# One tile for both parts of the tokens, packed gate jobs, and another order of exponentials, silus and scans, in a hybrid SSD and RG-LRU block

## The chip, the cores and the metric

The kernel runs on one core of one Trainium2 chip. The metric is the device time of one execution in microseconds; of several runs the median is given.

## The reference, cut to what matters

One layer over 256 latent and 256 context tokens, 2048 channels, all in float32. Tokens are normalised, modulated and projected once; the projection feeds two mixers, whose outputs are merged by gates taken from the same normalised tokens.

```python
h = modulate(rmsnorm(x, norm_mix), sh_m, sc_m)          # the context tokens alike
z, xs, bs, cs, dt_raw, xr, yr = split(h @ w_in)
xs, bs, cs = silu(conv4([xs, bs, cs]))                  # depthwise, 4 taps
dt = softplus(dt_raw + bias)
y  = bidirectional_ssd(xs, dt, A, bs, cs)               # 4 groups of 8 heads, chunks of 128
o_s = rmsnorm(y * silu(z)) @ w_out_ssd
r, i = sigmoid(xr @ w_a + b_a), sigmoid(xr @ w_x + b_x) # per head of 128, both directions
a = exp(-8 * r * softplus(-lam))
u = sqrt(1 - a * a) * (i * xr)
r_out = linear_scan(a, u)                               # both directions
o_r = (r_out * gelu(yr)) @ w_out_lru
g_s, g_r = split(sigmoid(h @ w_gate + b_gate))
x = x + g_m * ((g_s * o_s + g_r * o_r) @ w_o)
x = x + g_f * swiglu(modulate(rmsnorm(x), sh_f, sc_f))
out = rmsnorm(x)
```

Only the scans' final states are taken from the context tokens. The gates, z and yr need latent tokens alone.

## The kernel before, in words

Channels lie on the partitions, tokens on the free axis. Every float32 product is made of parts in the faster float32r form: a value is split into a high part and a low part (the rest), for the tokens as for the weights, and three of the four partial products are summed in PSUM: high by high, high weight by low token, low weight by high token. `T1` holds the high parts of the 16 channel tiles, `T2` the low parts; in each, columns 0 to 255 are latent and 256 to 511 context tokens.

A `Job` is one block of 128 output channels, over 16 channel tiles (44 for the last FFN matrix). SP loads its weights in pieces of 8 tiles (512 KB), ACT rounds a piece to the high part (L173), DVE subtracts to the low part (L174); rings of four pieces. `product` issues the matmuls in one of these forms:
- "both": three matmuls of 512 columns for each tile (L188 to L190), latent and context;
- "lat": three of 256 columns (L192 to L194): the gate jobs (32) and the jobs of C (4);
- "packed": one of 512 columns, whose operand holds high and low parts of 256 tokens side by side, and one of 256 with the low weights (L206, L209), for z, yr, the output projections and the FFN. `halves` (L300) then adds the two halves of the PSUM bank: a copy on ACT, an add on DVE;
- "slab" (L228, L230): six FFN jobs together, and "last": the last job of a matrix.

For the packed form both parts have to lie in one tile. So, after the last job on context tokens, 16 DVE copies (L924, L925) put the low latent parts into the context half of `T1`.

The order of PE's work is written out: jobs in a list, and after each job the work that is due in its turn. `in_turn(n, f)` (L243) asks for `f` n turns later, 0 being the job under way; it is called from a job's evacuation, or from a turn (there, 0 is the next job). Besides, `step` (L287) takes the next entries of the list `bg` once per job. On ACT and DVE a planner orders instructions by estimated times and priorities; but `fn` (L105) keeps all of ACT's functions that need a table (Exp, Silu, Sigmoid, Sqrt, Tanh, Gelu) in the order in which the program calls them.

Stages: input and modulation (to about 146 us); gate jobs, two for each xr job, with the RG-LRU (`lru_batch`, two channel tiles per batch: operands, gates of the first tile, gates of the second, decays, scans) and the softplus of dt (`dt_evac`); four groups of SSD jobs, six jobs each (xs, C, xs, B, xs, xs); the last eight gate jobs, under which the last group is computed; z, yr, the output projections, w_o, FFN. 

Of an SSD group (`ssd_group`), after its last xs job: the silus of B, C and xs at once, in the evacuation (L705); then, by the tables LONG and SHORT (the last group), the transposes and states (`context_tokens` first), and four units (two half groups by two chunks), each with `fetch` (a broadcast DMA of cumulated decays, AC), `operands` (Exp of AC and of E, then G) and `products` (24 matmuls, L833). The unit of LONG's last column has its products in turn 7, that is one job after the next group's xs is complete. In `lru_batch` the scans of the batch before (Sqrt first, L555) have an entry of their own ahead of the gates.

LONG and SHORT (L692, L693) give, in this order, the turns of the three steps of the states, of the four products, fetches and operands; `todo` (L573) gives the entries of an RG-LRU batch, where an entry marked True is done together with the one behind it.

Of the kernel before, what the change touches and what calls it, by code (L numbers as in the profile page):

```python
# [14 lines left out]
P = 128  # L15
# [40 lines left out]
def hybrid_block(  # L56
# [38 lines left out]
    T1 = big.tile([P, KT, 2 * T], F32R, name="T1")  # L95
    T2 = big.tile([P, KT, 2 * T], F32R, name="T2")
# [80 lines left out]
    def product(job, after_piece):  # L177
# [5 lines left out]
        for k in range(job.kts):  # L183
            h, l = job.w[k // KP]
            wh, wl = h[:, k % KP, :], l[:, k % KP, :]
            s, e = k == 0, k == last
            if job.mode == "both":
                pe.matmul(ps, wh, T1[:, k, :], start=s, stop=False)  # L188
                pe.matmul(ps, wh, T2[:, k, :], start=False, stop=False)  # L189
                pe.matmul(ps, wl, T1[:, k, :], start=False, stop=e)  # L190
            elif job.mode == "lat":
                pe.matmul(ps[:, :T], wh, T1[:, k, :T], start=s, stop=False)  # L192
                pe.matmul(ps[:, :T], wh, T2[:, k, :T], start=False, stop=False)  # L193
                pe.matmul(ps[:, :T], wl, T1[:, k, :T], start=False, stop=e)  # L194
            elif job.mode == "narrow":

                pe.matmul(ps, wh, T1[:, k, :], start=s, stop=False)
                pe.matmul(ps, wh, T2[:, k, :], start=False, stop=e)
            elif job.mode == "last":
                a = job.act(k)  # L200
                pe.matmul(ps[:, :T], wh, a[:, :T], start=s, stop=False)
                pe.matmul(ps[:, :T], wh, a[:, T:], start=False, stop=False)
                pe.matmul(ps[:, :T], wl, a[:, :T], start=False, stop=e)
# [17 lines left out]
    def slab(job, after_piece):  # L221

        pss = [mm_ps("ps1") for _ in range(NF - 4)] + [ssd_ps("ps1") for _ in range(3)] + [lru_ps("ps1")]
        for k in range(KT):
            h, l = job.w[k]
            a = job.act(k)
            for n, ps in enumerate(pss):
                pe.matmul(ps, h[:, n, :], a, start=k == 0, stop=False, skip_group_check=True)  # L228
            for n, ps in enumerate(pss):
                pe.matmul(ps[:, T:], l[:, n, :], a[:, :T], start=False, stop=k == KT - 1, skip_group_check=True)  # L230
# [78 lines left out]
    def split(dst, src):  # L309

        act.copy(dst[:, :T], src)
        dve.tensor_sub(dst[:, T:], src, dst[:, :T].bitcast(F32))
# [196 lines left out]
    def lru_batch(tiles):  # L509
# [42 lines left out]
        def scans():  # L552
# [4 lines left out]
            for t in tiles:  # L557
# [15 lines left out]
        todo = [(False, [lambda: operands(t0)]), (False, before[:]), (False, [lambda: gates(t0), lambda: operands(t1)]),  # L573
                (False, []), (True, [lambda: gates(t1), decays])]
# [23 lines left out]
    def dt_evac(ps):  # L598
# [13 lines left out]
        def steps(part):  # L612
# [11 lines left out]
            if part == 0:  # L624
# [9 lines left out]
                fn(ex[:, :P], ex[:, :P], AF.Exp)  # L634
                dve.tensor_tensor(ex[f, :P], ex[f, :P], dt[f, 0:P], ALU.mult)
                dve.tensor_tensor(ex[b, :P], ex[b, :P], dt[b, P:2 * P], ALU.mult)
                cols = (dt[:, :P], dt[:, P:], ac[:, :P], ac[:, P:], ex[:, :P])
            else:
                scan(ex[f, :T - 1][:, ::-1], da[f, 1:][:, ::-1], T - 1, f)
                scan(ex[b, 1:], da[b, :T - 1], T - 1, b)  # L640
                fn(ex, ex, AF.Exp)
                dve.tensor_tensor(ex, ex, dt, ALU.mult)
                cols = (ex[:, :P], ex[:, P:])

# [66 lines left out]
    def ssd_group(g):  # L711
# [133 lines left out]
        return (silus, [context_tokens, context_states, carried_states], *zip(*units))  # L845
# [42 lines left out]
    def z_job(i):  # L888
        ys, pre = loads(yD[i])

        def f(ps):
# [5 lines left out]
            act.activation(T2[:, i, :T], t, AF.Copy, scale=g)  # L897
            dve.scalar_tensor_tensor(T2[:, i, T:], t, g, T2[:, i, :T].bitcast(F32), ALU.mult, ALU.subtract)
        return Job(w_z[i], KT, "packed", h_act, f, pre=pre)

    def yr_job(i):
        rs, pre = loads(rD[i])

        def f(ps):
# [3 lines left out]
            split(T3[:, i, :], t)  # L908
        return Job(w_yr[i], KT, "packed", h_act, f, pre=pre)

    def h_act(k):
        return T1[:, k, :]
# [4 lines left out]
    with tc.manual_schedule(engines={mybir.EngineType.PE}):  # L917
# [4 lines left out]


        for k in range(KT):  # L924
            dve.tensor_copy(T1[:, k, T:], T2[:, k, :T].bitcast(F32))  # L925
# [15 lines left out]
    def mix_jobs(n):  # L941
# [11 lines left out]
        def fr(ps):  # L953
# [3 lines left out]
            split(T1[:, n, :], t)  # L957

        return [Job(w_os[n], KT, "packed", lambda k: T2[:, k, :], fs, pre=pre),
                Job(w_ol[n], KT, "packed", lambda k: T3[:, k, :], fr)]  # L960
# [15 lines left out]
    def f_act(k):  # L976
        t = (T2, T3, T4)[k // KT]
        return t[:, k % KT, :]
# [44 lines left out]
    for k in range(KT):  # L1023
# [4 lines left out]
        dve.scalar_tensor_tensor(T1[:, k, T:], t, sh, T1[:, k, :T].bitcast(F32), ALU.add, ALU.subtract)  # L1028
# [94 lines left out]
```

## Time and profile before

| what | value |
|---|---|
| three runs | 2028.81, 2029.35, 2024.41 us, median 2028.81 |
| profiled execution | 2027.59 us, span 2025.8 us |
| PE busy | 1963.7 us, 97% |
| DVE busy | 1430.7 us, 71% |
| ACT busy | 1088.2 us, 54% |
| mean granted clock of PE | 0.986 of 2.4 GHz |
| ACT table loads | 48, 1283 ns each |

A matmul's listed duration holds its way through the array, which the next one overlaps; what one costs in a row of matmuls is the distance from start to start. A granted clock of 1.00 is 2.4 GHz, 0.50 is 1.2 GHz; a value between is a mix of both within the stretch. In a timeline's brackets stands the idle time of the engine ahead of an instruction, and what released it.

### The profile page before, as it was taken

The numbers are of one execution on the slowest core, as the hardware profiler recorded it, in microseconds if no ns is written. First come the engines' busy times: TensorE is split into PE (matmuls) and PEld (weight loads), VectorE is DVE, ScalarE is ACT, GpSimd is POOL, SyncE is SP. The second block draws the span as 40 slices with busy tenths as digits, with TensorE's granted clock in tenths as the row PEclk, the third lists the DMA queues.
The fourth block names the chain that finished last, engine by engine and source line by source line (L and its number), as shares of the span: only waits on it lengthen the run. The fifth ranks groups of instructions, "written<-read, shape, count | busy, mean of one in ns | idle before, by whom it ended". The sixth has DMA issues, their size and how long they took to land.

```text
span 2025.8 us, 30510 instructions
## 1 busy us (share of the span) xinstructions
PE 1963.7 (97%) x11633; PEld 1691.9 (84%) x11633; DVE 1430.7 (71%) x2153; ACT 1088.2 (54%) x1652; POOL 0.2 (0%) x4
## 2 busy tenths in 40 slices
PE   7999899999999879999999999899999999999997
PEld 3778898898878769888888888788888888888887
DVE  5578989886776666888777878776666665545544
ACT  4245878684564454766655544554444444444442
POOL 0000000000000000000000000000000000000000
PEclk9999999999999989999999999999999999999999
DMA  9974354556454457899888877577777776666663
GB/s 371 358 271 144 122 160 132 170 170 199 140 160 143 138 164 228 264 315 360 290 274 274 271 249 254 175 249 232 231 241 237 230 230 189 184 188 186 185 193 122
DMA packets 143842, 440.32 MB, mean 217 GB/s; under 512 B 17488, under 2 KB 36176, under 8 KB 143568
## 3 DMA queue, kind: packets, MB, share of 16 engines
q1 hardware_dynamic: 143328, 437.91, 66.4%
q8 instruction: 91, 1.49, 0.3%
q10 hardware_dynamic: 368, 0.47, 0.1%
q14 instruction: 55, 0.45, 0.1%
HBM read 427.77 MB, written 10.55 MB: 216 GB/s over the span
## 4 chain that ended last, share of the span: by engine, by line
PE 92%; DMA 2%; DVE 2%; ACT 2%; issue 1%; SPq 0%; DVEq 0%; ACTq 0%
PE ps L206 36%; PE ps L209 19%; PE ps L188 5%; PE ps L189 5%; PE ps L190 5%; PE ps L192 3%; PE ps L193 3%; PE ps L194 3%; DMA AC<-acD 1%; PE ps L391 1%; PE pa L344 1%; PE ps L392 1%; PE py L833 1%; PE ps L393 1%; PE ps L228 1%; PE lg L535 1%
## 5 line engine op out<-in xcount | busy, mean ns | idle before, releaser
L174 DVE TENSOR_TENSOR wl<-raw,wh 128x1024 fp32r<-128x1024 f32 (+1 forms) x566 | 677.8, 1200 | 386.9 <-ACT wh L173 382.3
L173 ACT CAST wh<-raw 128x1024 fp32r<-128x1024 f32 (+1 forms) x566 | 581.0, 1030 | 646.8 <-issue 221.4
L206 PE MATMUL ps<-T,wh 128*128 128x512 f32 x3236 | 814.7, 393 | 0.0
L206 PEld LDWEIGHTS ps<-T,wh 128*128 128x128 f32 x3236 | 581.6, 189 | 105.2 <-issue 0.7
L209 PEld LDWEIGHTS ps<-T,wl 128*128 128x128 f32 x3236 | 442.7, 190 | 33.3
L209 PE MATMUL ps<-T,wl 128*128 128x256 f32 x3236 | 452.9, 282 | 0.0
L188 PE MATMUL ps<-T,wh 128*128 128x512 f32 x464 | 184.2, 397 | 0.0
L189 PE MATMUL ps<-T,wh 128*128 128x512 f32 x464 | 180.9, 390 | 0.0
L190 PE MATMUL ps<-T,wl 128*128 128x512 f32 x464 | 180.6, 389 | 0.0
L473 DVE SCALAR_TENSOR_TENSOR rawa<-rawa,sc 128x1024 f32<-128x1024 f32 x128 | 153.1, 1222 | 28.4 <-DMA rawa<-in_dram 28.1
L192 PE MATMUL ps<-T,wh 128*128 128x256 f32 x576 | 165.4, 287 | 0.0
L193 PE MATMUL ps<-T,wh 128*128 128x256 f32 x576 | 163.7, 284 | 0.0
L194 PE MATMUL ps<-T,wl 128*128 128x256 f32 x576 | 163.6, 284 | 0.0
L192 PEld LDWEIGHTS ps<-T,wh 128*128 128x128 f32 x576 | 111.3, 193 | 1.9 <-issue 0.7
L193 PEld LDWEIGHTS ps<-T,wh 128*128 128x128 f32 x576 | 111.4, 193 | 1.2 <-issue 0.5
L194 PEld LDWEIGHTS ps<-T,wl 128*128 128x128 f32 x576 | 111.2, 193 | 0.0
L188 PEld LDWEIGHTS ps<-T,wh 128*128 128x128 f32 x464 | 87.1, 188 | 20.5 <-issue 2.3
L189 PEld LDWEIGHTS ps<-T,wh 128*128 128x128 f32 x464 | 87.2, 188 | 18.9 <-issue 1.4
L190 PEld LDWEIGHTS ps<-T,wl 128*128 128x128 f32 x464 | 87.1, 188 | 18.5
L107 ACT ACT_TABLE_LOAD x48 | 61.6, 1283 | 0.8
L804 ACT ACTIVATE E<-AC,wt 128x128 f32<-128x128 f32 x64 | 20.6, 391 | 61.8 <-DMA AC<-acD 61.8
L385 DVE TENSOR_TENSOR wl<-raw,wh 128x896 fp32r<-128x896 f32 x16 | 17.5, 1092 | 45.1 <-ACT wh L384 45.1
(236 smaller groups left out, 1881.8 us busy)
## 6 DMA issues: line engine op xcount, KB each, us to landing
raw<-in_dram SPq DMA_DIRECT2D x534, 512.0 KB, 4.5
rawa<-in_dram SPq DMA_DIRECT2D x128, 512.0 KB, 5.9
wa<-in_dram SPq DMA_DIRECT2D x64, 512.0 KB, 7.2
AC<-acD SPq DMA_DIRECT2D x16, 512.0 KB, 6.6
raw<-in_dram SPq DMA_DIRECT2D x16, 448.0 KB, 7.1
raw<-in_dram SPq DMA_DIRECT2D x16, 384.0 KB, 3.3
raw<-in_dram SPq DMA_DIRECT2D x18, 256.0 KB, 2.7
X<-in_dram SPq DMA_DIRECT2D x8, 512.0 KB, 7.2
```

Of the source, the lines that this page charges most:

```text
L107: i = act.activation(dst, src, func, **kw).ins
L173: act.copy(h[:, :n], raw[:, :n])
L174: held["low"] = dve.tensor_sub(l[:, :n], raw[:, :n], h[:, :n].bitcast(F32)).ins
L188: pe.matmul(ps, wh, T1[:, k, :], start=s, stop=False)
L189: pe.matmul(ps, wh, T2[:, k, :], start=False, stop=False)
L190: pe.matmul(ps, wl, T1[:, k, :], start=False, stop=e)
L192: pe.matmul(ps[:, :T], wh, T1[:, k, :T], start=s, stop=False)
L193: pe.matmul(ps[:, :T], wh, T2[:, k, :T], start=False, stop=False)
L194: pe.matmul(ps[:, :T], wl, T1[:, k, :T], start=False, stop=e)
L206: pe.matmul(ps, wh, job.act(k), start=s, stop=False, skip_group_check=True)
L209: pe.matmul(ps[:, T:], l[:, i % KP, :], job.act(i)[:, :T], start=False, stop=i == last, skip_group_check=True)
L473: i = dve.scalar_tensor_tensor(raw, raw, 1.0, sc[:, h * 1024:h * 1024 + 1024], ALU.mult, ALU.mult, accum_out=MP[:, n, h:h + 1]).ins
```

## The change

- `T1` and `T2` become the two halves of one tile `TT`. The packed form reads an operand of two strips of 256 columns, one in each half (`h_act`, `c_act`), in place of 512 adjacent columns; the matmul's output is still one bank of 512 columns.
- The gate jobs take the packed form, and `halves`. The 16 copies go. z's result is put into the context columns of both halves.
- An RG-LRU batch's scans come behind the next batch's gates of the first tile, in that entry, and no longer in the entry ahead.
- The dt work starts one turn later, and its exponentials and transposes get turns of their own.
- The silus of an SSD group move from the evacuation into turn 0, behind what that turn holds already; in the last group but one the fourth unit's products move from turn 7 to 8.

```diff
-    T1 = big.tile([P, KT, 2 * T], F32R, name="T1")
-    T2 = big.tile([P, KT, 2 * T], F32R, name="T2")
+    TT = big.tile([P, 2, KT, 2 * T], F32R, name="TT")
+    T1, T2 = TT[:, 0], TT[:, 1]
...
-                pe.matmul(ps, wh, job.act(k), start=s, stop=False, skip_group_check=True)
+                pe.matmul(ps.rearrange("p (s t) -> p s t", s=2), wh, job.act(k), start=s, stop=False,
+                          skip_group_check=True)
...
-                        pe.matmul(ps[:, T:], l[:, i % KP, :], job.act(i)[:, :T], start=False, stop=i == last,
+                        pe.matmul(ps[:, T:], l[:, i % KP, :], job.act(i)[:, 0], start=False, stop=i == last,
...
+    def h_act(k):
+        return TT[:, :, k, :T]
+    def c_act(k):
+        return TT[:, :, k, T:]
+    def pair(t, k):
+        return t[:, k, :].rearrange("p (s t) -> p s t", s=2)
     def gate_evac(n):
         def f(ps):
-            t = tp.tile([P, T], F32, tag="hv", name="gt", bufs=4)
-            act.copy(t, ps[:, :T])
-            side.dma_start(gD[n], t)
+            side.dma_start(gD[n], halves(ps, "gt"))
...
-        return Job(w_gate[n], KT, "lat", None, gate_evac(n))
+        return Job(w_gate[n], KT, "packed", h_act, gate_evac(n))
...
-        todo = [(False, [lambda: operands(t0)]), (False, before[:]), (False, [lambda: gates(t0), lambda: operands(t1)]),
-                (False, []), (True, [lambda: gates(t1), decays])]
+        todo = [(False, [lambda: operands(t0)]), (False, []),
+                (False, [lambda: gates(t0), lambda: operands(t1)] + before), (False, []), (True, [lambda: gates(t1), decays])]
...
+            def weights():
+                if part == 0:
+                    fn(ex[:, :P], ex[:, :P], AF.Exp)
...
+                else:
+                    fn(ex, ex, AF.Exp)
+                    dve.tensor_tensor(ex, ex, dt, ALU.mult)
...
-            return turn
-
-        def first():
-            turn0()
-            in_turn(4, steps(1))
-
-        turn0 = steps(0)
-        in_turn(4, first)
+                else:
+                    return
+                begin(1)
+
+            in_turn(1, weights)
+            in_turn(3, turn)
+
+        def begin(part):
+            in_turn(1, lambda: steps(part))
+
+        begin(0)
...
-    LONG = ((1, 2, 3), (4, 5, 6, 7), (2, 3, 4, 5), (3, 4, 5, 6))
-    SHORT = ((2, 3, 5), (7, 9, 11, 13), (4, 6, 7, 9), (5, 7, 9, 11))
+    LONG = ((0,), (1, 2, 3), (4, 5, 6, 7), (2, 3, 4, 5), (3, 4, 5, 6))
+    LAST_LONG = LONG[:2] + ((4, 5, 6, 8),) + LONG[3:]
+    SHORT = ((0,), (2, 3, 5), (7, 9, 11, 13), (4, 6, 7, 9), (5, 7, 9, 11))
...
-                silus, *rest = ssd_group(g)
-                silus()
-                for ns, fs in zip(LONG if g < NG - 1 else SHORT, rest):
+                when = LONG if g < NG - 2 else LAST_LONG if g < NG - 1 else SHORT
+                for ns, fs in zip(when, ssd_group(g)):
...
-            act.activation(T2[:, i, :T], t, AF.Copy, scale=g)
-            dve.scalar_tensor_tensor(T2[:, i, T:], t, g, T2[:, i, :T].bitcast(F32), ALU.mult, ALU.subtract)
+            act.activation(T1[:, i, T:], t, AF.Copy, scale=g)
+            dve.scalar_tensor_tensor(T2[:, i, T:], t, g, T1[:, i, T:].bitcast(F32), ALU.mult, ALU.subtract)
...
-        for k in range(KT):
-            dve.tensor_copy(T1[:, k, T:], T2[:, k, :T].bitcast(F32))
```

## Rows read from the trace of the kernel before

**Rows 1.** Stretches: length, busy us (instructions) by engine, clock, DMA share, GB/s.
```profile
146.00:505.00 359.00, 351.80 (x2102) 314.52 (x2101) 303.12 (x378) 257.24 (x358) 0.00 (x0) 0.99 0.50 155
505.00:738.00 233.00, 221.58 (x1218) 179.81 (x1217) 167.33 (x306) 124.93 (x216) 0.00 (x0) 0.97 0.50 148
738.00:845.00 107.00, 93.51 (x696) 85.18 (x695) 76.22 (x130) 60.78 (x101) 0.00 (x0) 0.92 0.68 219
1300.00:1800.00 500.00, 500.00 (x2865) 439.85 (x2864) 319.10 (x428) 247.10 (x365) 0.00 (x0) 1.00 0.69 223
```

**Rows 2.** Timeline of PE: start, duration, engine, line, names, count, idle before.
```profile
199.26 0.50 PE L535 MATMUL lg<-xh,lh 128*128 128x512 f32 x1 [1.89 <-ACT R L107]
...
220.69 0.80 PE L535 MATMUL lg<-xh,lh 128*128 128x512 f32 x1 [5.32 <-ACT R L107]
...
588.13 0.70 PE L833 MATMUL py<-G,xt 128*64 128x128 f32 x4 [5.05 <-DVE G L816]
...
671.77 0.69 PE L833 MATMUL py<-G,xt 128*64 128x128 f32 x4 [6.37 <-DVE G L816]
...
754.61 0.70 PE L833 MATMUL py<-G,xt 128*64 128x128 f32 x4 [11.62 <-DVE G L816]
...
841.80 0.44 PE L833 MATMUL py<-G,xt 128*64 128x128 f32 x4 [1.88 <-DVE G L816]
```

**Rows 3.** Busy time in stretches of 2 us around those waits.
```profile
202.00:204.00 2.00, 2.00 (x7) 1.61 (x7) 0.81 (x3) 1.99 (x4) 0.00 (x0) 0.50 0.00 0
...
592.00:594.00 2.00, 2.00 (x15) 2.00 (x14) 1.10 (x3) 1.94 (x5) 0.00 (x0) 0.70 0.71 123
...
674.00:676.00 2.00, 2.00 (x17) 1.67 (x14) 0.71 (x4) 0.51 (x2) 0.00 (x0) 0.72 0.09 22
...
760.00:762.00 2.00, 2.00 (x17) 2.00 (x16) 0.00 (x0) 0.22 (x1) 0.00 (x0) 0.89 0.83 247
```

**Rows 4.** Timeline of ACT around the third and the fifth of those waits.
```profile
564.10 1.28 ACT L804 ACTIVATE E<-AC,wt 128x128 f32<-128x128 f32 x4 [1.01 <-DMA AC<-acD]
...
581.94 1.92 ACT L107 ACTIVATE XS<-XS 128x2048 f32<-128x2048 f32 x1 [0.93 <-DVE XS L448]
583.86 1.28 ACT L107 ACT_TABLE_LOAD   x1
585.16 1.06 ACT L107 ACTIVATE AC<-AC 128x1024 f32<-128x1024 f32 x1
...
748.43 1.91 ACT L107 ACTIVATE XS<-XS 128x2048 f32<-128x2048 f32 x1 [1.31 <-DVE XS L448]
```

**Rows 5.** Timeline of DVE, the last taps of XS.
```profile
575.30 0.75 DVE L448 SCALAR_TENSOR_TENSOR XS<-pad,V,XS 128x512 f32<-128x512 f32 x1
579.23 1.23 DVE L805 SCALAR_TENSOR_TENSOR E<-AC,wt,E 128x128 f32<-128x128 f32 x4 [3.17 <-ACT E L804]
580.38 1.53 DVE L448 SCALAR_TENSOR_TENSOR XS<-pad,V,XS 128x512 f32<-128x512 f32 x2
```

**Rows 6.** Timeline of ACT in the RG-LRU stretch.
```profile
196.79 0.42 ACT L107 ACTIVATE dt<-dt 64x256 f32<-64x256 f32 x1 [3.95 <-DVE dt L614]
...
217.49 1.15 ACT L107 ACTIVATE E<-E,epsb 128x1024 f32<-128x1024 f32 x1 [1.15 <-DVE E L549]
218.65 1.28 ACT L107 ACT_TABLE_LOAD   x1
```

**Rows 7.** Timeline of PE, gate job (L194) and packed jobs.
```profile
175.01 0.28 PE L194 MATMUL ps<-T,wl 128*128 128x256 f32 x1
...
176.81 0.28 PE L194 MATMUL ps<-T,wl 128*128 128x256 f32 x1
...
1500.47 2.00 PE L206 MATMUL ps<-T,wh 128*128 128x512 f32 x8
...
1503.26 2.00 PE L206 MATMUL ps<-T,wh 128*128 128x512 f32 x8
```

**Rows 8.** By line, 800 to 880 us: count, busy us, mean ns, idle before.
```profile
L306 DVE TENSOR_TENSOR zt<-ps,zt 128x256 f32<-128x256 f32 x10 | 4.2, 424 | 0.0
```

More of the change, by code (lines that the diff above doesn't have):

```diff
@@ L200, in product @@
                 a = job.act(k)
-                pe.matmul(ps[:, :T], wh, a[:, :T], start=s, stop=False)
-                pe.matmul(ps[:, :T], wh, a[:, T:], start=False, stop=False)
-                pe.matmul(ps[:, :T], wl, a[:, :T], start=False, stop=e)
-            else:
-                pe.matmul(ps, wh, job.act(k), start=s, stop=False, skip_group_check=True)
+                pe.matmul(ps[:, :T], wh, a[:, 0], start=s, stop=False)
+                pe.matmul(ps[:, :T], wh, a[:, 1], start=False, stop=False)
+                pe.matmul(ps[:, :T], wl, a[:, 0], start=False, stop=e)
+            else:
+                pe.matmul(ps.rearrange("p (s t) -> p s t", s=2), wh, job.act(k), start=s, stop=False,
+                          skip_group_check=True)
                 if k % KP == KP - 1 or e:
                     for i in range(k - k % KP, k + 1):
-                        pe.matmul(ps[:, T:], l[:, i % KP, :], job.act(i)[:, :T], start=False, stop=i == last,
+                        pe.matmul(ps[:, T:], l[:, i % KP, :], job.act(i)[:, 0], start=False, stop=i == last,
                                   skip_group_check=True)
@@ L227, in slab @@
             for n, ps in enumerate(pss):
-                pe.matmul(ps, h[:, n, :], a, start=k == 0, stop=False, skip_group_check=True)
+                pe.matmul(ps.rearrange("p (s t) -> p s t", s=2), h[:, n, :], a, start=k == 0, stop=False,
+                          skip_group_check=True)
             for n, ps in enumerate(pss):
-                pe.matmul(ps[:, T:], l[:, n, :], a[:, :T], start=False, stop=k == KT - 1, skip_group_check=True)
+                pe.matmul(ps[:, T:], l[:, n, :], a[:, 0], start=False, stop=k == KT - 1, skip_group_check=True)
             if k < KT - 1:
@@ L309, in split @@
     def split(dst, src):
-        act.copy(dst[:, :T], src)
-        dve.tensor_sub(dst[:, T:], src, dst[:, :T].bitcast(F32))
+        act.copy(dst[:, 0], src)
+        dve.tensor_sub(dst[:, 1], src, dst[:, 0].bitcast(F32))
     def rstd_of(ps, n, name, pool=tp):
@@ L640, in steps @@
                 scan(ex[b, 1:], da[b, :T - 1], T - 1, b)
-                fn(ex, ex, AF.Exp)
-                dve.tensor_tensor(ex, ex, dt, ALU.mult)
                 cols = (ex[:, :P], ex[:, P:])
+            def weights():
+                if part == 0:
+                    fn(ex[:, :P], ex[:, :P], AF.Exp)
+                    dve.tensor_tensor(ex[f, :P], ex[f, :P], dt[f, 0:P], ALU.mult)
+                    dve.tensor_tensor(ex[b, :P], ex[b, :P], dt[b, P:2 * P], ALU.mult)
+                else:
+                    fn(ex, ex, AF.Exp)
+                    dve.tensor_tensor(ex, ex, dt, ALU.mult)
             def turn():
@@ L844, in ssd_group @@
         units = [unit(u, c) for u in range(2) for c in range(2)]
-        return (silus, [context_tokens, context_states, carried_states], *zip(*units))
+        return ([silus], [context_tokens, context_states, carried_states], *zip(*units))
     jobs = [Job(w_dt, KT, "narrow", None, dt_evac)]
@@ L907, in f @@
             dve.tensor_tensor(t, t, rs[0], ALU.mult)
-            split(T3[:, i, :], t)
+            split(pair(T3, i), t)
         return Job(w_yr[i], KT, "packed", h_act, f, pre=pre)
-    def h_act(k):
-        return T1[:, k, :]
     z_jobs = [z_job(i) for i in range(KT)]
@@ L956, in fr @@
             dve.tensor_tensor(t, t, o, ALU.add)
-            split(T1[:, n, :], t)
-        return [Job(w_os[n], KT, "packed", lambda k: T2[:, k, :], fs, pre=pre),
-                Job(w_ol[n], KT, "packed", lambda k: T3[:, k, :], fr)]
+            split(h_act(n), t)
+        return [Job(w_os[n], KT, "packed", c_act, fs, pre=pre),
+                Job(w_ol[n], KT, "packed", lambda k: pair(T3, k), fr)]
     def wo_evac(i):
@@ L976, in f_act @@
     def f_act(k):
-        t = (T2, T3, T4)[k // KT]
-        return t[:, k % KT, :]
+        return c_act(k) if k < KT else pair((T3, T4)[k // KT - 1], k % KT)
     def ffn_jobs(n):
@@ L1027, in hybrid_block @@
         act.activation(T1[:, k, :T], t, AF.Identity, bias=sh)
[L1028 removed]
+        dve.scalar_tensor_tensor(T2[:, k, :T], t, sh, T1[:, k, :T].bitcast(F32), ALU.add, ALU.subtract)
     del held["ra"]
```

3 lines of the change are left out of this document (removed).

## The prediction

> **What bounds the kernel now.** I first read the busy time by stretch. In each, PE is the fullest engine, and from 1300 to 1800 us it has work all the time at a granted clock of 1.00 [rows 1]; nothing of the change makes that part shorter, unless its matmuls cost another time. So what is to be had lies in two things: where PE stands still, and how many columns it streams. Between 146 and 845 us its busy time falls 7, 11 and 13 us short of the three stretches, and only there is the clock below 1.00 for reasons that the change touches [rows 1].
>
> Then the timeline of PE, for those holes. Six matmuls there have a wait in brackets [rows 2]. The first two stand in the RG-LRU stretch: a gate product whose PSUM bank is still being read by a sigmoid on ACT. The next three are the fourth unit of SSD groups 0, 1 and 2, waiting for G, which DVE makes from an Exp; they are the largest: 5.05, 6.37 and 11.62 us. The last, 1.88 us, is the last unit of group 3.
>
> Why they are late is in ACT's timeline. The fourth unit's decays are in E's input at 564.1 us, long before PE needs them; but its Exp of AC runs at 585.2, behind the silu of the next group's xs (581.9 to 583.9) and a table load [rows 4]. The program calls the silus in the evacuation of the next group's last xs job, ahead of that turn's remaining exponentials, and ACT keeps that order. The silu itself waits for the last two taps of the convolution, which DVE has put behind a step on the decays of yet another unit [rows 5]. In group 2 the chain is the same and longer: the silu comes at 748.4 [rows 4]. In the RG-LRU stretch likewise: the Exp of the second dt part at 196.8 stands ahead of a sigmoid, and later the Sqrt of a batch's scans, itself waiting for DVE, plus a table load [rows 6].
>
> **After a wait the clock is down.** In the pieces of 2 us behind the waits PE runs at 0.50, and within 592 to 594, 674 to 676 and 760 to 762 it comes back, mixed clocks 0.70, 0.72 and 0.89 [rows 3]. So 1.2, 1.1 and 0.4 us of those pieces were still slow. PE's work from 588.13 to 593.2, from 671.77 to 675.1 and from 754.61 to 760.4 ran at half speed: 5.1, 3.3 and 5.8 us, of which half is lost: 2.5 + 1.7 + 2.9 = 7.1 us. Behind the first RG-LRU wait 3.4 us ran at half (0.50 in 202 to 204, and the edges), which loses 1.7; I take the same for the second.
>
> **The change part by part.**
>
> *Silus behind the exponentials, products of group 2 one turn later.* Now the fourth unit's Exp can follow its E step at 564 us, some 19 us before PE wants the products. The three waits go: 5.05 + 6.37 + 11.62 = 23.0 us, and 7.1 of clock. What is late next: `context_tokens`, which follows at once for groups 1 and 2 and needs the silu of xs. That silu keeps its own wait for the taps. It ended at 583.9; PE was free at 588.13 - 5.05 = 583.1, and has the 24 products and the transposes of B first. For group 3, PE was free at 754.61 - 11.62 = 743.0; one more gate job (16 x 0.349 = 5.6 us, below) brings it to 748.6, products come first, and the silu ended at 748.43 + 1.91 = 750.3. So the next wait is at most 0.8 to 1.7 us each if the silu stays where it was, and I allow 3 x 1.7 = 5 us for the three, which also stands for smaller shifts that the planner makes. The silu may also come earlier: the Exps no longer follow it. The group's number of table loads stays: Exp, Silu, Exp.
>
> *Scans behind the gates, dt in later turns.* The sigmoids no longer stand behind the Sqrt and its wait, nor behind a dt Exp of the same turn: 1.89 + 5.32 = 7.2 us and 2 x 1.7 = 3.4 of clock. The price: Sqrt now falls between the sigmoids of a batch's two tiles, so each of the 7 batches that have an earlier one to scan has one table load more, 7 x 1.28 = 9.0 us of ACT [rows 6]. Queued behind a load on ACT are the weight roundings and PSUM copies; PE has up to four weight pieces in its rings. ACT is busy 257 of 359 us there [rows 1]; with 9 more in a stretch that becomes some 15 us shorter, 266 of 344, it has room, so I cost it at nothing; without cover it would be 9 us. The Trainium skill speaks against this edit: its page "ScalarE: Activation LUTs", section "Table sets: the hidden batching unit", asks for all calls of one table set before the next, and prices a switch at about 2.7 us with its drain. The trace has 1.30 us from the load's start to the next function's start (583.86 to 585.16) [rows 4], so the measurement decides; by the page's figure the 7 loads would cost ACT some 19 us, an estimate, which the idle time would cover still.
>
> *Gate jobs packed.* A gate job's triple takes (176.81 - 175.01) / 5 = 0.360 us, the packed pair (1503.26 - 1500.47) / 8 = 0.349 [rows 7]: both stream 768 columns, and only an instruction's fixed part is saved. 32 jobs x 16 x 0.0112 = 5.7 us. It adds a DVE step of 0.424 us per gate [rows 8]; 24 of them fall into the RG-LRU stretch: 303 + 10 = 313 us of DVE in 344, 91%. The remaining 9% and the rings hide it; were that gone, it is rival 2. The gate's store on SP leaves half a microsecond later, and nobody reads it for hundreds of microseconds.
>
> *No copies.* 16 short DVE instructions in the last xs job of group 3 go. PE waits for none of them; they stand among the taps of xs, so the gain is within the allowance. At nothing.
>
> *Two strips in one operand.* 3236 packed matmuls of 512 columns, 96 of the slab and the 512 new ones read their operand as two runs of 256 columns. The trace has no such operand. Below, nothing can be gained: the columns are the same. Above, the break could at worst empty the array once: a lone matmul of 256 columns lasts 0.28 us where a following one adds 0.12 [rows 7], that is 0.16 us. The nearest row is the triple, whose matmuls change between tiles `T1` and `T2` from one to the next in equal steps of 0.12 us, so a jump of address costs nothing there, and I take nothing. The page "SBUF — State Buffer" of the Trainium skill, at the end of its section "Door 1: The DMA port swizzle", has a penalty only where accesses keep leaving a line of 16 bytes, and slow matmuls for PSUM patterns that aren't contiguous; runs of 1 KB and an output of 512 adjacent columns would cost nothing by it. No row here shows that.
>
> **The sum.** 23.0 + 7.1 + 7.2 + 3.4 + 5.7 = 46.4 us, less 5 of allowance: 41. From the profiled execution's 2027.6 this leaves 1986; the median of the runs is 1.2 above it, so 1987.
>
> **Rivals.**
> 1. *The silu's wait takes the place.* For it: the taps stand behind a DVE step that waits for decays to land (3.17 us idle at 579.2) [rows 5], and the margins above are under 2 us. Against it: the Exps and their table load leave ACT's queue at that point. If at each of the three places a wait of the size of the first (5.05 us) with its 2.5 of clock remains, 22.6 us are not gained, the allowance being part of that: 1987 + 22.6 - 5 = 2005.
> 2. *The RG-LRU stretch becomes DVE's.* For it: 91% busy, scans and dt pushed to later turns, and a planner that orders by its own estimates. Against it: DVE had 84% without PE waiting for weights. Then this stretch keeps its length: 7.2 + 3.4 + 24/32 of 5.7 = 15 us are lost: 2002.
> 3. *Slower: the strip break costs PE time.* 3844 matmuls; from 41 / 3844 = 10.7 ns each all is eaten, and at 15 ns, an eighth of a step of 256 columns, it is 58 us: 2045. For it: no row shows such an operand. Against it: the equal steps above. It would show in the packed stretch, which nothing else touches.
> 4. *False order.* With both parts in one tile, a planner that took the read of two strips for all that lies between them would make each z, yr, output and FFN job wait for the evacuation of the one before: four steps of 0.42 us in some 90 jobs, 150 us, about 2140. The parts of `T1` were told apart before, so I give it little.
> 5. *It doesn't do what it says:* new orders on DVE or SP make the same products late (a later AC, say), and only the gates are gained: 2022.
>
> **How the numbers follow.** The forecast 0.58, rival 1 0.18, rival 2 0.10, rival 3 0.07, rival 4 0.02, rival 5 0.05. The first case alone has 1976 to 1996: below, the allowance unused and the sixth wait (1.88 and its slow clock, as much again) gone with it; above, twice the allowance and more. The range reaches over rivals 1 and 2, with some of both: 1975 to 2012. A measurement of this kernel can tell some 0.3%, 6 us, from no change. Faster 0.85 (the first three, and half of the last), slower 0.10 (rivals 3 and 4, and a rest), no change 0.05.
>
> **What would show it.** In the changed kernel's timeline of PE the waits for G at a group's end are gone, ACT has the fourth unit's Exps before the silus of B, C and xs, and the clock is 1.00 through 500 to 760 us, save for a wait of 1 to 2 us ahead of the transposes of xs. In the gate jobs a pair takes 0.349 us, and in the packed stretch eight pairs still take 2.79 us: if that distance has grown, rival 3 has it. ACT has about 7 table loads more. DVE between 146 and 490 us is near 90% and no weight piece is late. The forecast is wrong if a wait for XS or for weights of more than 3 us stands where the old ones were, or if the stretch after 850 us takes another time than before.

## The result, and the profile after

The changed kernel takes 2004.73 us (median of four runs, 2003.33 to 2006.08), the kernel before 2029.08 beside it: a ratio of 0.9885, interval 0.9868 to 0.9902. The gain is 24 us. I had said 41, to 1987: the time lies in the range, near what rival 1 gives (2005) and rival 2 (2002), and it will turn out that a part of each came.

The profiled execution took 2006.08 us, its span 2004.2. First the busy time and then the table loads (count, total, mean), from parts 1 and 5 of the page of the changed kernel:

```profile
PE 1955.7 (98%) x11121; PEld 1661.9 (83%) x11121; DVE 1434.7 (72%) x2169; ACT 1098.0 (55%) x1660; POOL 0.2 (0%) x4
```

```profile
L108 ACT ACT_TABLE_LOAD x56 | 71.8, 1283 | 1.6 <-PE lg L547 0.7
```

There are 8 loads more than before; I had 7. Then what PE waits for, in total, how often, and the longest:

```profile
PE ssq L335 <- DVE sq L334: 8.9, 6, 7.1
PE pt L662 <- DVE dt L657: 8.6, 1, 8.6
PE px L753 <- ACT XS L108: 6.7, 2, 3.7
PE ps L230 <- DVE TT L1037: 4.5, 1, 4.5
PE pa L356 <- ACT ra L354: 2.7, 2, 1.6
PE ps L189 <- DVE gt L309: 2.6, 2, 2.3
PE pa L347 <- DMA wa<-in_dram: 1.4, 4, 0.6
PE rs L892 <- ACT sqt L885: 1.3, 2, 0.7
PE ps L207 <- DVE gt L309: 1.1, 1, 1.1
```

None of the six matmuls of [rows 2] is in it: no `py` waits for G, no `lg` for R. Three kinds of wait are new: the transposes of dt (`pt`, 8.6 us), the transposes of xs (`px`, 6.7), and a matmul whose PSUM bank is still being read by a gate's add on DVE (`gt`, 1.1 + 2.6). In PE's timeline (columns as in [rows 2]) the larger ones stand here:

```profile
225.51 2.08 PE L207 MATMUL ps<-TT,wh 128*128 128x512 f32 x8 [1.06 <-DVE gt L309]
...
248.20 0.47 PE L662 MATMUL pt<-K,dt 64*128 64x64 f32 x2 [8.55 <-DVE dt L657]
...
662.90 1.97 PE L753 MATMUL px<-K,XS 128*128 128x128 f32 x8 [3.03 <-ACT XS L108]
...
744.41 1.97 PE L753 MATMUL px<-K,XS 128*128 128x128 f32 x8 [3.69 <-ACT XS L108]
```

The stretches that answer to [rows 1], shorter by what was gained, and pieces of 2 us behind the three longest waits (length, busy us by engine, clock, DMA share, GB/s):

```profile
146.00:490.00 344.00, 331.77 (x1655) 281.44 (x1654) 300.95 (x391) 263.16 (x362) 0.00 (x0) 0.99 0.51 157
490.00:720.00 230.00, 226.97 (x1227) 184.29 (x1226) 168.00 (x291) 120.71 (x205) 0.00 (x0) 0.99 0.50 154
720.00:825.00 105.00, 101.31 (x636) 85.83 (x635) 84.65 (x152) 70.72 (x119) 0.00 (x0) 0.97 0.76 238
...
250.00:252.00 2.00, 2.00 (x6) 1.57 (x5) 0.55 (x1) 1.98 (x4) 0.00 (x0) 0.50 0.00 0
...
666.00:668.00 2.00, 2.00 (x11) 2.00 (x11) 1.77 (x3) 1.64 (x3) 0.00 (x0) 0.50 0.57 85
...
748.00:750.00 2.00, 2.00 (x7) 1.61 (x6) 2.00 (x6) 2.00 (x7) 0.00 (x0) 0.50 0.88 198
```

PE is below its stretch by 12, 3 and 4 us, before by 7, 11 and 13. So the SSD groups have been nearly cleared and the RG-LRU stretch got worse. Behind these three waits the clock is at 0.50 again, and that loses some 2.0, 2.9 and 2.9 us; behind the gate's add at 225.51 it is 1.00 (226 to 230).

**Where the 24 us come from.** Three marks of the two traces split the span: the first transpose of B (`pB`, the start of the SSD groups), the last `py`, and the slab's start.

| stretch, in us | before | after | gain | forecast |
|---|---|---|---|---|
| start to first `pB` | 509.7 | 509.3 | 0.4 | 7.2 + 3.4 + 4.3 = 14.9 |
| first `pB` to last `py` | 333.1 | 312.2 | 20.9 | 23.0 + 7.1 + 1.4 - 5 = 26.5 |
| last `py` to slab | 429.7 | 428.3 | 1.4 | 0 |
| slab to end | 753.3 | 754.4 | -1.1 | 0 |

(4.3 and 1.4 are the gates' 5.7, by 24 and 8 jobs.) The RG-LRU stretch gave nothing of its 15 us, and the SSD stretch 6 less than its term. In what follows "the first mark" is the start of the SSD groups in a kernel's one profiled execution. The input stage, which none of the edits is meant to change, ends at different times in these executions: the first gate job starts between 145.35 and 149.12 us. So the table also has the time from the first gate job to the first mark, the length of the RG-LRU stretch.

### The profile page after: what moved, and what is told of

Same layout as the page of the kernel before. It is cut to its first block, busy times and chain, and to the rows that moved or that the text cites. A ratio compares the mean times of both kernels' runs of the same rounds, so it can differ in the third digit from the quotient of the medians.

```text
span 2004.2 us, 29578 instructions
## 1 busy us (share of the span) xinstructions
PE 1955.7 (98%) x11121; PEld 1661.9 (83%) x11121; DVE 1434.7 (72%) x2169; ACT 1098.0 (55%) x1660; POOL 0.2 (0%) x4
## 4 chain that ended last, share of the span: by engine, by line
PE 90%; DVE 4%; ACT 3%; DMA 2%; issue 1%; DVEq 0%; SPq 0%; ACTq 0%
PE ps L207 41%; PE ps L211 21%; PE ps L189 5%; PE ps L190 5%; PE ps L191 5%; PE ps L394 1%; PE ps L230 1%; PE ps L395 1%; PE pa L347 1%; PE ps L396 1%; DMA AC<-acD 1%; PE py L850 1%; DMA wa<-in_dram 1%; DVE wl L175 1%; PE ps L233 1%
## 5 line engine op out<-in xcount | busy, mean ns | idle before, releaser
L207 PE MATMUL ps<-TT,wh 128*128 128x512 f32 x3072 | 772.6, 393 | 1.1 <-DVE gt L309 1.1
L207 PEld LDWEIGHTS ps<-TT,wh 128*128 128x128 f32 x3072 | 554.4, 189 | 103.7 <-issue 3.5
L211 PEld LDWEIGHTS ps<-TT,wl 128*128 128x128 f32 x3072 | 419.7, 191 | 30.3
L211 PE MATMUL ps<-TT,wl 128*128 128x256 f32 x3072 | 429.0, 282 | 0.0
L189 PE MATMUL ps<-TT,wh 128*128 128x512 f32 x464 | 185.3, 399 | 2.6 <-DVE gt L309 2.6
L190 PE MATMUL ps<-TT,wh 128*128 128x512 f32 x464 | 181.5, 391 | 0.0
L191 PE MATMUL ps<-TT,wl 128*128 128x512 f32 x464 | 181.2, 390 | 0.0
L207 PE MATMUL ps<-T,wh 128*128 128x512 f32 x676 | 172.2, 394 | 0.0
L207 PEld LDWEIGHTS ps<-T,wh 128*128 128x128 f32 x676 | 120.8, 188 | 21.8
L189 PEld LDWEIGHTS ps<-TT,wh 128*128 128x128 f32 x464 | 87.5, 189 | 23.8 <-issue 4.4
L190 PEld LDWEIGHTS ps<-TT,wh 128*128 128x128 f32 x464 | 87.6, 189 | 19.0 <-issue 1.4
L191 PEld LDWEIGHTS ps<-TT,wl 128*128 128x128 f32 x464 | 87.5, 189 | 18.7
L211 PEld LDWEIGHTS ps<-T,wl 128*128 128x128 f32 x676 | 93.5, 189 | 8.2
L211 PE MATMUL ps<-T,wl 128*128 128x256 f32 x676 | 95.7, 281 | 0.0
L821 ACT ACTIVATE E<-AC,wt 128x128 f32<-128x128 f32 x64 | 20.5, 391 | 62.1 <-DMA AC<-acD 62.1
L394 PE MATMUL ps<-TT,wh 128*128 128x512 f32 x112 | 46.6, 416 | 0.0
L395 PE MATMUL ps<-TT,wh 128*128 128x512 f32 x112 | 43.8, 391 | 0.0
```

The source lines that it names most:

```text
L207: pe.matmul(ps.rearrange("p (s t) -> p s t", s=2), wh, job.act(k), start=s, stop=False, skip_group_check=True)
L211: pe.matmul(ps[:, T:], l[:, i % KP, :], job.act(i)[:, 0], start=False, stop=i == last, skip_group_check=True)
L394: pe.matmul(ps0[n], h[:, n, :], T1[:, k, :], start=k == 0, stop=False)
L395: pe.matmul(ps0[n], h[:, n, :], T2[:, k, :], start=False, stop=False)
L821: act.activation(E[:, h], AC[:, 0, h], AF.Identity, bias=wt[:, 2 + c, hf:hf + 1])
```

## The experiments

| kernel | median us | ratio to before, interval | first gate job to first mark | first mark | from there to the end |
|---|---|---|---|---|---|
| before | 2029.08 | | 363.7 | 509.7 | 1516.1 |
| after | 2004.73 | 0.9885, 0.9868 to 0.9902 | 363.0 | 509.3 | 1494.9 |
| silus alone | 2003.68 | 0.9881, 0.9868 to 0.9895 | 364.0 | 511.2 | 1488.9 |
| layout and gates alone | 2022.46 | 0.9979, 0.9969 to 0.9989 | 362.8 | 510.2 | 1508.1 |
| scans and dt back | 2003.72 | 0.9877, 0.9862 to 0.9892 | 362.8 | 510.2 | 1491.0 |
| scans back | 1998.46 | 0.9855, 0.9842 to 0.9868 | 356.9 | 506.0 | 1492.5 |
| dt back | 2005.93 | 0.9890, 0.9875 to 0.9905 | 366.6 | 512.8 | 1492.1 |
| dt's transposes later | 2002.27 | 0.9873, 0.9859 to 0.9886 | 361.0 | 506.3 | 1493.0 |
| squares on ACT | 2008.50 | 0.9903, 0.9886 to 0.9919 | 366.9 | 515.4 | 1491.2 |
| gate's add first | 2005.53 | 0.9887, 0.9873 to 0.9902 | 363.3 | 510.6 | 1489.7 |
| E in the tables' order | 2000.43 | 0.9863, 0.9849 to 0.9876 | 363.2 | 510.9 | 1486.7 |
| scans back, transposes later, add first, E in order | 1992.93 | 0.9829, 0.9815 to 0.9843 | 356.9 | 503.6 | 1486.6 |
| the same, and squares on ACT | 1992.11 | 0.9820, 0.9805 to 0.9835 | 355.2 | 503.0 | 1489.9 |

The kernel before was run again beside the others. Its median was 2027.30 us beside silus alone, layout alone, scans back and dt back; 2027.23 beside transposes later, add first, E in order and the four together; 2029.46 beside the other three. What an edit saves against it is taken from that median. An interval reaches some 3 us to either side, so a difference of 2 or 3 us between two changed kernels is not told from nothing.

**Silus alone.** The kernel before, with the edit of the silus and its tables of turns, and nothing else:

```diff
-                silus, *rest = ssd_group(g)
-                silus()
-                for ns, fs in zip(LONG if g < NG - 1 else SHORT, rest):
+                when = LONG if g < NG - 2 else LAST_LONG if g < NG - 1 else SHORT
+                for ns, fs in zip(when, ssd_group(g)):
```

> The kernel before with the new place of the silus and the new turn tables alone; layout, gate jobs, scans and dt as before. Theory A (the trace of the changed kernel: the waits for G go, 5.05 + 6.37 + 11.62 us and 7 us of slow clock, and waits of the transposes for the silu of xs come, 6.7 us and about 6 of clock): 30 - 13 = 17 us faster than before, so about 2012. Rival B (the SSD groups' gain needs the copies to be gone too, since they stand among the taps of xs): the wait ahead of the transposes of group 3 is longer than 3.7 us by the copies' 4 us and more, gain below 12 us, 2017 or more.

It saves 23.6 us, as much as the whole change, and more than the 17 that I expected. The `py` waits are gone but for 0.5 us, so the mechanism of the forecast's largest term needs neither the tile nor the turns of dt. Only one `px` wait, of 3.3 us, came here, and in the stretches of 490 to 720 and 720 to 825 us the clock is 1.00 nevertheless. Then the other four parts together are worth nothing that these runs can tell.

**Layout and gates alone.** The changed kernel with the silus, the scans and dt as before:

```diff
-        todo = [(False, [lambda: operands(t0)]), (False, []),
-                (False, [lambda: gates(t0), lambda: operands(t1)] + before), (False, []), (True, [lambda: gates(t1), decays])]
+        todo = [(False, [lambda: operands(t0)]), (False, before[:]), (False, [lambda: gates(t0), lambda: operands(t1)]),
+                (False, []), (True, [lambda: gates(t1), decays])]
...
-                for ns, fs in zip(when, ssd_group(g)):
+                silus, *rest = ssd_group(g)
+                silus()
```

> The changed kernel with the orders of before (silus in the evacuation, scans ahead of the gates, dt as before); one tile for both parts, packed gate jobs and no copies stay. Theory A (PE gains the fixed part of one instruction of each triple, 512 x 11.2 ns, and gives back part of it to waits for the DVE addition of the gates): 0 to 6 us faster than before, 2023 to 2029. Rival B (the two strips cost PE time): the distance of eight packed pairs is above 2.79 us, and the time above 2035. Rival C (the additions make the RG-LRU stretch DVE's): waits for the gate's addition of 5 us and more, 2030 to 2040.

It saves 4.9 us, against 5.7 forecast for the gates. But its first mark is where it was: 24 gate jobs of the RG-LRU stretch should have brought it 4.3 us forward. In their place PE there waits 8.7 us for sigmoids (7.2 before) and 2.2 for a gate's add, which the kernel before doesn't have. What was gained lies behind the first mark, where only 8 of the 32 gate jobs stand, and part of it is in the waits for G: 22.3 us in place of 24.9, with the sixth of [rows 2] gone. That 4.9 is close to 5.7 is chance.

**Scans and dt back.** The changed kernel with both as before, so silus and layout stay:

> The changed kernel with both moves of the RG-LRU stretch undone (scans and dt as before); silus, layout, packed gates stay. Theory A (the parts add up: silus 23.6 and layout 4.9 us in their own runs): 2027.3 - 28.5 = 1999, that is, the two moves together make the changed kernel 6 us slower. Rival B (dt's move is worth what its waits cost before, 7.2 us and slow clock, and only the scans' move harms): about 2005, as slow as with dt alone undone.

Its median is that of the silus alone to 0.04 us, near the rival's 2005. On top of the silus the layout brings nothing that can be told: 23.6 and 4.9 saved singly, 25.7 together. The rows of PE's waits say what the gates' 5.7 us went into: beside the silus alone, 2.2 more for the gate's add and 2.4 more for `px` (5.7 against 3.3). The clock is 0.50 behind the gate's add (432 to 434 us) and 0.63 behind the longer `px` wait (666 to 668), but 1.00 behind the other (744 to 748).

```profile
PE lg L545 <- ACT R L108: 8.6, 2, 5.1
PE px L746 <- ACT XS L108: 5.7, 2, 3.8
PE ps L230 <- DVE TT L1030: 4.5, 1, 4.5
PE pa L356 <- ACT ra L354: 3.1, 2, 2.0
PE ps L207 <- DVE gt L309: 2.2, 1, 2.2
PE p L776 <- DVE xw L739: 2.0, 1, 2.0
```

**Scans back.** The changed kernel with its entries of an RG-LRU batch as before (the `todo` lines of the diff above), dt as changed:

> The changed kernel with the scans back in an entry of their own ahead of the gates. Theory A (the move took away a wait of a gate product for a sigmoid behind Sqrt, 5.3 us and 2 of clock, at the cost of idle ACT time): 7 us slower than the changed kernel, about 2012, seven table loads fewer. Rival B (the move only shifted DVE's backlog into the wait of the dt transposes, 8.55 us): the dt wait shrinks by as much as the old one returns, 2002 to 2006.

The result is 6 us faster than the changed kernel. I had not expected that. No sigmoid wait returns, so those two waits go by the later turns of dt alone, and the move of the scans only costs: it makes 6 of the 8 added table loads (here there are 50), and it puts more DVE work ahead of dt's transposes. The second dt part's steps on DVE, from the first behind its Exp to the last product, take 33.6 us here, 39.4 in the changed kernel and 16.8 before. The wait of the transposes is 4.11 us here, 8.55 in the changed kernel.

**dt back.** The changed kernel with dt's steps and turns as before, scans behind the gates:

> The changed kernel with the dt steps as before (first part in the evacuation, transposes four turns later, the second part likewise). Theory A (the wait of 8.55 us of the second part's transposes comes from its later start, into the stretch where DVE is full): it goes with its 2 us of clock and the sigmoid wait of 1.9 us and 1.7 of clock returns: 7 us faster than the changed kernel, about 1998. Rival B (DVE's load decides, whenever the dt work starts): a wait of about the same 8 to 10 us stands elsewhere between 190 and 260 us, 2002 to 2008.

It takes the time of the changed kernel, as the rival had it: a wait of one kind for a wait of another. The `pt` wait is gone, one sigmoid wait is back (3.55 us at 200.41), and the other has become a wait for ACT's copy out of PSUM, in PE's and ACT's timelines:

```profile
235.82 3.78 PE L207 MATMUL ps<-TT,wh 128*128 128x512 f32 x8 [5.73 <-ACT pad L443]
```

```profile
233.78 0.72 ACT L108 ACTIVATE A<-R,SL 128x512 f32<-128x512 f32 x1 [1.44 <-DVE E L571]
234.41 0.62 ACT L308 COPY gt<-ps 128x256 f32<-128x256 f32 x2
234.93 0.63 ACT L441 COPY pad<-ps 128x256 f32<-128x256 f32 x1
235.34 0.43 ACT L443 COPY pad<-ps 128x256 f32<-128x256 f32 x1
```

The copies stand behind the decays (`A<-R,SL`), and these wait for the scan on DVE (L571) of the batch before, which now comes late. So the four corners of the two edits, with silus and layout in place, are 2003.7 (neither), 1998.5 (dt), 2005.9 (scans) and 2004.7 (both); only the corner with dt alone has runs clear of the others' (1996.26 to 2000.28; theirs begin at 2002.91).

**dt's transposes later.** Only the second part's (`part` is 1), 9 turns later and not 3:

```diff
-            in_turn(3, turn)
+            in_turn(3 if part == 0 else 9, turn)
```

> The changed kernel, only with the second dt part's transposes ten jobs behind its steps instead of four. Theory A (PE stood 8.55 us in its written order ahead of transposes whose DVE steps came late; nothing else needs them there): the wait and 2 us of slow clock go, 10 us faster than the changed kernel, about 1994. Rival B (DVE's backlog is a matter of rate, and the next consumer of its work waits in place of the transposes): waits for the gate's addition or for weights grow by 5 us and more, and the time stays above 2000.

The 8.55 us wait is gone, but the median gains 2.5, not 10: the wait moves on. A gate product waits 0.95 us at 264.62, and then a job's first matmul longer, in PE's timeline:

```profile
272.13 0.79 PE L189 MATMUL ps<-TT,wh 128*128 128x512 f32 x1 [4.70 <-DVE gt L309]
```

**Squares on ACT.** To take load from DVE, a batch's a*a goes to ACT:

```diff
-                dve.tensor_tensor(E, A, A, ALU.mult)
+                act.activation(E, A, AF.Square)
```

> The changed kernel, only with the squares of the decays (E = A * A, 1.22 us each on DVE, 32 in all) made by ACT as Square, 1.15 us each, which needs no table. Theory A (DVE is full between 205 and 250 us, and all that waits there, dt's transposes, gate additions, waits for its backlog): with some 19 us of DVE gone from that stretch the dt wait of 8.55 us falls below 3 and the gate waits of 3.7 us go: 8 to 12 us faster than the changed kernel, 1993 to 1997. Rival B (the order decides, not the load): the dt wait stays at 7 us or more, 2002 to 2006. Rival C (ACT becomes the late one, at 281 of 344 us): waits for weights or sigmoids come, 2005 or more.

This costs 3.8 us. From 146 to 490 us DVE falls by 16.7 us and ACT rises by 13.1:

```profile
146.00:490.00 344.00, 332.10 (x1638) 281.36 (x1637) 284.21 (x376) 276.22 (x377) 0.00 (x0) 0.98 0.49 155
```

The `pt` wait falls to 6.2 us only, and the waits for a gate's add rise from 3.7 to 5.8. DVE's load alone is thus not what holds PE. In that stretch DVE waits more for ACT: 4.7 us for the squares, 20.5 in place of 13.8 for the rounded weights of the gate products (`lh`), and 16.9 in place of 11.5 for the other rounded weights (`wh`).

**Gate's add first.** A high priority for a gate's copy and add:

```diff
-            side.dma_start(gD[n], halves(ps, "gt"))
+            with tc.high_priority(500):
+                t = halves(ps, "gt")
+            side.dma_start(gD[n], t)
```

> The changed kernel, only with the copy and the addition that empty a gate job's PSUM bank put ahead of other work by priority. Theory A (the bank waits for DVE only by the planner's order): the waits for the gate's addition, 1.06 + 2.6 us, go: 3 to 4 us faster, about 2001; the dt wait may grow by as much as the additions come ahead of its steps, under 1 us. Rival B (DVE is full, so what is put ahead is taken from the dt steps): the dt wait of 8.55 us grows by 3 us or more, no gain.

Inconclusive: the median is that of the changed kernel, and the waits are the same ones (1.05, 2.6 and 8.57 us). It was not ACT's copy that held the adds back: in the changed kernel the copies end at 222.4 and 450.5, and the adds that PE waits for start at 224.96 and 454.20, behind other work on DVE. With the priority DVE has the same instructions ahead of the first of them; why the planner did not move it I have not found out.

**E in the tables' order.** The step that makes E's input from AC, and so waits for AC's landing, is called through `fn`, behind the functions ahead of it in the program (among them the silu of xs):

```diff
-                    act.activation(E[:, h], AC[:, 0, h], AF.Identity, bias=wt[:, 2 + c, hf:hf + 1])
+                    fn(E[:, h], AC[:, 0, h], AF.Identity, bias=wt[:, 2 + c, hf:hf + 1])
```

> The changed kernel, only with ACT's first step on a unit's decays (Identity into E, which waits for AC to land) tied into the order of the table functions, so that a unit of the next group can't stand ahead of the silu of xs. Theory A (the silu of xs is late because ACT, and behind it DVE's last taps, wait for decays that land 5 to 7 us after their issue): the waits of the transposes, 6.7 us and some 6 us of slow clock, go: 10 to 13 us faster than the changed kernel, about 1993. Rival B (it is late because DVE has the two sums for adaLN, 2.4 us, ahead of the taps): at least 4 of the 6.7 us stay, above 1999.

It gains 4.3 us where I expected 10 to 13 (8.2 behind the first mark in the profiled executions), and the `px` waits fall from 6.7 to 0.7 us. This is the cause of those waits. In the changed kernel ACT and DVE stand, in this order (timelines of each, around the first of the two):

```profile
657.79 1.28 ACT L821 ACTIVATE E<-AC,wt 128x128 f32<-128x128 f32 x4 [7.21 <-DMA AC<-acD]
658.98 1.03 ACT L174 CAST wh<-raw 128x1024 fp32r<-128x1024 f32 x1
660.94 1.91 ACT L108 ACTIVATE XS<-XS 128x2048 f32<-128x2048 f32 x1 [0.93 <-DVE XS L451]
```

```profile
658.23 1.23 DVE L822 SCALAR_TENSOR_TENSOR E<-AC,wt,E 128x128 f32<-128x128 f32 x4 [4.07 <-ACT E L821]
659.37 1.53 DVE L451 SCALAR_TENSOR_TENSOR XS<-pad,V,XS 128x512 f32<-128x512 f32 x2
```

ACT does nothing for 7.21 us but wait for AC; DVE waits for ACT for 4.07 of them; behind DVE's step stand the last two taps of xs, and behind those the silu. With E in order, the silu has already started at 657.17 and AC's step follows it (ACT's timeline, then the busy time from 490 to 720 us):

```profile
657.17 1.92 ACT L108 ACTIVATE XS<-XS 128x2048 f32<-128x2048 f32 x1 [2.72 <-DVE XS L451]
659.80 1.28 ACT L108 ACTIVATE E<-AC,wt 128x128 f32<-128x128 f32 x4 [0.71 <-DMA AC<-acD]
```

```profile
490.00:720.00 230.00, 230.00 (x1254) 186.66 (x1253) 171.76 (x301) 125.30 (x218) 0.00 (x0) 1.00 0.52 157
```

In that stretch PE is without a gap, at 1.00. What is paid for it are 2.7 us for G and 1.3 for `xw` later.

**Scans back, transposes later, gate's add first, E in order.** These four edits together:

> The changed kernel with the scans back ahead of the gates (1998.5 in its own run), and the three edits of e1, e2 and e3. Theory A (each takes away a wait of its own place): from 1998.5 less 4.1 + 2 us (dt), less 4.1 + 2.0 us and 4 of clock (transposes for xs, states for xw), less 2.2 (gates): 1980 to 1985. Rival B (the waits are one backlog of DVE in the RG-LRU stretch and one chain in the groups, which move on): at most half of it, above 1990.

1992.93 us, 12 less than the changed kernel and a version that beats both, and above 1990. The single gains against the changed kernel (6.3, 2.5 and 4.3) sum to 13, but that they nearly add is not a proof that each of them came: the RG-LRU stretch is 356.9 us, as with the scans back alone, so behind those the later transposes seem to bring nothing, and the rest of the gain lies behind the first mark (1486.6 in place of 1492.5), where E in order acts. From 200 to 250 us PE is now full at 1.00; the wait has moved on to a gate's add, 2.94 us at 255.21, and there is a second further on (5.2 together).

**The same with the squares on ACT.**

> The kernel of e8 (1992.9) with the squares on ACT. Theory A (DVE's load): its waits for gate additions, 5.2 us and 2 of clock, go: 1986. Rival B or C of the run with the squares alone: 1991 or more.

1992.11: the intervals of the two lie over each other, and the waits for the gates' adds are 5.0. Here the squares neither cost nor bring anything that can be told.

## Why the prediction was right, and where it was wrong

The direction, and the place of the largest gain, were right; the size was not, and the two steps that failed are the first two below. By the sign that I had set myself (a wait for XS of more than 3 us where the old ones were) the forecast of 41 us is wrong: there were two, 3.03 and 3.69 us. That the time falls on rival 1's 2005 is chance, since about half of rival 1's loss and nearly all of rival 2's came together. And the chances that I added for faster (the first three and half of the last) make 0.885, not 0.85.

**Silus behind the exponentials: right, with the allowance too small.** All four waits for G of [rows 2] are gone, the last too, as the first case's lower end had it, and the edit alone gives 23.6 of the 24 us. I had written that "the next wait is at most 0.8 to 1.7 us each if the silu stays where it was", and allowed 5 us for three. Two came, 3.03 and 3.69 us, and their slow clock cost about 5.8 more: 12.5 us in the profiled execution. The chain that I read in [rows 5], taps behind a DVE step that waits for ACT's step on AC, was the right one; I priced the silu by where it had stood at groups 0 and 2, each wait by itself, and did not ask where AC would land once the earlier waits were gone. ACT had stood as long at the same step before, in front of the same silu, and nobody waited for it, since PE waited for G (ACT's timeline of the kernel before):

```profile
662.45 1.28 ACT L804 ACTIVATE E<-AC,wt 128x128 f32<-128x128 f32 x4 [7.46 <-DMA AC<-acD]
665.59 1.91 ACT L107 ACTIVATE XS<-XS 128x2048 f32<-128x2048 f32 x1 [0.93 <-DVE XS L448]
```

In the changed kernel PE comes to that group's products at 657.31, and before it was free for them at 671.77 - 6.37 = 665.40: 8.1 us earlier. ACT's step on AC starts 4.7 us earlier (657.79 for 662.45), and so does the silu. Before, PE would have come to `px` at about 668.0 (2.6 us of products and transposes of B stand ahead of it) and the silu was done at 667.5, so some 0.4 us were to spare; the 3.4 us by which PE got ahead of ACT, less these, are the new wait of 3.03. E in order, which takes the silu out from behind that step, shows it. So of rival 1's 22.6 us 12.5 came, at two of its three places.

**Scans behind the gates, dt in later turns: "I cost it at nothing" is the step that failed.** 10.6 us were to come from it, and the first mark stands where it stood. The old waits did go. But the path to PE was not the sigmoid alone: from 205 to 248 us DVE is busy for 41.6 of 43 us, and in the changed kernel its last piece is the second part's dt chain, for which PE's next matmul waits (timelines of DVE, and the Exp in ACT's):

```profile
233.75 0.41 DVE L144 SCALAR_TENSOR_TENSOR dt<-dt,dt 64x256 f32<-64x256 f32 x1
...
245.87 1.37 DVE L624 TENSOR_TENSOR_SCAN dt<-dt,dtx 32x255 f32<-32x255 f32 x2
247.72 0.42 DVE L657 TENSOR_TENSOR dt<-dt,dt 64x256 f32<-64x256 f32 x1 [0.48 <-ACT dt L108]
```

```profile
247.28 0.42 ACT L108 ACTIVATE dt<-dt 64x256 f32<-64x256 f32 x1 [7.49 <-DVE dt L624]
```

Seven steps of this chain, of the kind of the first line, are spread from there to 243.8 us. Before, the same seven ran in one row (DVE's timeline):

```profile
188.67 1.32 DVE L143 SCALAR_TENSOR_TENSOR dt<-dt,dt 64x256 f32<-64x256 f32 x3
190.02 1.77 DVE L143 SCALAR_TENSOR_TENSOR dt<-dt,dt 64x256 f32<-64x256 f32 x4
```

I counted ACT's room (266 of 344 us; measured 263) and DVE's share (313; measured 301) over the whole stretch, and both counts were about right. What they can't show is the order in 40 us in which DVE is full: it was as full there before (43.0 of the 43 us). In the changed kernel the dt chain is spread between scans, weights and gates over 39.4 us in place of 16.8, and PE comes to its transposes before it is done. I named the instructions queued behind the table loads, not those behind the moved scans. Of the two edits the one on dt is worth 5 us on top of silus and layout, and the scans' costs 6 beside dt (and 2 alone, which can't be told from nothing). A rule of the Trainium skill ("ScalarE: Activation LUTs", section "Table sets: the hidden batching unit") had spoken against the scans' move. The result agrees with its advice, but that the loads are the reason is not shown; and its price of about 2.7 us a switch is not borne out, since a load takes 1.283 us here and the next function starts 1.30 us after the load does (568.72 to 570.02 in the changed kernel). At dt's wait it is DVE's order: ACT, which makes the loads, stands idle there for 7.49 us. For the rest of the 6 us I can't tell the loads and DVE's order apart: scans back undoes both.

**Gate jobs packed: the pitch was right, the cover was not.** The first four gate-job pieces of eight pairs start at 146.33, 149.10, 151.89 and 154.68, 0.35 us a pair as forecast. But the term was for PE's columns, and in the RG-LRU stretch it was eaten by new waits; the 4.9 us of the layout alone lie elsewhere. I had written that DVE's remaining time and the rings hide the add; the rings hold weights, and the add has a PSUM bank to free as well. With the step above this is rival 2's place and price, 14.5 of its 15 us, though the squares on ACT show that DVE's load alone is not its mechanism.

**Two strips, false order: as forecast.** The packed stretch of the changed kernel, whose eight pairs I wanted at 2.79 us as in [rows 7]:

```profile
1481.71 2.00 PE L207 MATMUL ps<-TT,wh 128*128 128x512 f32 x8
1483.55 1.12 PE L211 MATMUL ps<-TT,wl 128*128 128x256 f32 x8
1484.50 2.00 PE L207 MATMUL ps<-TT,wh 128*128 128x512 f32 x8
```

1484.50 - 1481.71 = 2.79. The break in the operand costs nothing, and rival 3 is out. No output job waits for the one before, and the slab to the end takes 1.1 us more, which is within what the profiled executions differ by (753.0 to 754.5): rival 4 is out. Rival 5 is out with the silus alone.

**The sum again.** Of 46.4 us, 10.6 (scans, dt) and the gates' 4.3 didn't come, nor 7.5 of the allowance's other side (12.5 - 5), while the sixth wait (1.88 and as much for clock) came on top. 41 - 10.6 - 4.3 - 7.5 + 3.8 = 22.4, beside 21.5 between the two profiled executions and 24.3 between the medians.

**What stays open.** The dt edit was not run on the kernel before by itself, nor with the silus alone in the old layout. The silus' new place and the later turn of group 2's products were not run apart, nor the scans back with E in order and nothing else. Open are also why AC's landing came forward less than PE, why the priority moved nothing, and how much of the scans' cost is table loads.

## What to carry to other kernels

Follow each wait that is taken away to the next matmul in PE's order, and ask there what its input's engine stands on at that moment, in the window and not over the stretch. On an engine that works in order, a step that waits for a DMA belongs behind the critical function, not ahead of it. And measure the parts of a change singly and in pairs: here one part was worth the whole, and of two others one gained 5 us only without the other, whose undoing gave 6 us.

## What was not expected of the hardware

- The clock after a wait of PE: in the changed kernel 0.50 after 3.03 us, back within 668 to 670 (mixed 0.85); with the squares on ACT the same two waits, 6.3 us together, left both SSD stretches at 1.00. In scans and dt back a wait of 2.24 us (to 431.83) has 0.50 behind it, and in silus alone one of 3.30 (to 665.10) has 1.00. The length of a wait alone doesn't tell whether it is paid twice.
- ACT stood idle ahead of its steps on AC for 62.1 us in all in the changed kernel, and for 61.8 before. The same wait for a landing costs nothing while PE waits for something else, and is paid when PE comes earlier.
